# An encoder step on one core: every low-part subtraction of the output projections and of the plain gate/up tiles on VectorE

## Chip, cores and metric

The kernel runs on one NeuronCore of a Trainium2 chip (core 0, 16 DMA engines). The metric is the device time of one execution in microseconds. The median of three runs before the change is 2269.16 us (2268.02 to 2269.37). Engines in the text: TensorE (PE, with PEld for its weight loads), VectorE (DVE), ScalarE (ACT), GpSimd (POOL) and SyncE (SP), which issues the DMAs.

## The reference

Two layers run over 1056 rows (1024 prompt rows and 32 sample rows) of width 1024. Layer 0 mixes with an mLSTM, layer 1 with windowed attention with sinks and ALiBi; each has an output projection, a SwiGLU feed-forward part of width 2816 and two DeepNorm layer norms.

```python
def swiglu(x, w_gu, w_down):
    g, u = jnp.split(x @ w_gu, 2, axis=-1)
    return (jax.nn.silu(g) * u) @ w_down
...
for layer in range(DEPTH):
    if layer < N_A_LAYERS:
        mix, C, n, m = mlstm_mixer(x, w_in_a[layer], b_gate_a[layer], g_norm_a[layer], w_out_a[layer],
                                   C0s[layer], n0s[layer], m0s[layer])
    else:
        mix = swa_prompt(x, k_sh, v_sh, w_q_b[j], sinks_b[j], w_out_b[j], slopes)
    x = layer_norm(DEEPNORM_ALPHA * x + mix, ln_g[layer, 0], ln_b[layer, 0])
    x = layer_norm(DEEPNORM_ALPHA * x + swiglu(x, w_gu[layer], w_down[layer]), ln_g[layer, 1], ln_b[layer, 1])
```

## The kernel before

Activations lie transposed (feature on the partition) in `ACT` ("act" in the profile), 8 tiles of 128 features by 1056 columns. A product is formed from fp32r high and low parts: for every pair of tiles `gemm` issues three matmuls, high by high (L360), high by low (L361) and low by high (L362). `SX` ("sx") holds high and low parts of the activations; `split_act` makes them (ACT copies the high part at L390, DVE subtracts at L391), or the layer norm does (ACT L468; then L474, for even pairs of tiles on DVE, for odd ones on POOL).

Weights come through the class `Weights`. A unit is a tile of 128 x 1024; `load_to` issues its DMA on SP into one of three raw buffers ("wr", L159). Each unit has two halves, called factors 0 and 1, of 128 x 512. `_next` does the next half in a fixed order: ACT copies the high part (L200, into "wh"), then one engine subtracts it from the raw tile to give the low part (L202, into "wl"; or "ex"/"oh" where the half has a home in another buffer). This subtraction is called a split below. The engine of a split is chosen by one line: VectorE if (unit, factor) is in the set `on_vector`, GpSimd otherwise. Halves without a home share five slots. Most feed-forward tiles are in pairs with seven Strassen-like factors ("wl_a", "wl_b", "wl_s"), which the change does not touch.

`_next` is called while matmuls are written: `Weave.tick` counts the TensorE time issued so far and calls `feed`, and `split_to`/`factor` call it where a half is needed. The schedule is manual, so the order of the program text is the order on each engine's queue, and every engine runs its queue strictly in order.

Places at which the change acts:

- `mixer_out` with `U_OUT_A` (L1135 adds its products to act), after the mLSTM; `proj_o` with its chain of ACT L1034, DVE L1038, ACT L1040 and L1041, DVE L1043, L1044 and L1046 ends just before it, and its results are split at L390 and L391.
- `attention` with its stages scores (PE L1669/L1670, DVE L1675), soft (ACT L1687, DVE L1691, POOL L1693), turn (PE transposes L1713, ACT L1716, DVE L1717 writes "lo"), values (PE L1728/L1729), place (ACT L1737, DVE L1739). `mixer_out` with `U_OUT_B` begins while attention still runs.
- `up_plain`: the first FIRST = 2 gate/up tiles of each layer, once for each half of the columns (ACT silu L1251, DVE L1253). Meanwhile `ln_task` finishes the layer norm (DVE L426, L430, L447, L448, L452; POOL some of L430 and L474; PE L421 and L437), and `sums` makes sums of activations (DVE L1287 to L1293, ACT L1277, then L1274 alternating between POOL and DVE).

## Time and profile before

| | |
|---|---|
| median of 3 runs | 2269.16 us |
| the profiled execution | 2261.86 us |
| its span, first to last instruction | 2259.8 us |
| mean granted TensorE clock | 0.996 |
| DVE busy | 1490.3 us (66%) |
| ACT busy | 1015.3 us (45%) |
| POOL busy | 1135.6 us (50%) |

Durations below come from that one profiled execution. A row of the timeline gives the start in us from the span's start, the time in us, engine, line and operation, output and inputs, shapes and count, and in brackets the idle time of the engine before it and what ended it. In the table of waits a row reads: who waited, for whom, us in total, times, longest.

### The profile page before, as it was taken

Reading aid. Unit: us, or ns where it says so; the run is one execution under the profiler, and the core shown is the slowest. Engines: PE = TensorE matmul, PEld = TensorE weight load, DVE = VectorE, ACT = ScalarE, POOL = GpSimd, SP = SyncE. Lnnn points to the kernel's source line nnn. Section 1 sums busy time; section 2 is a strip of 40 time slices with the busy share of each in tenths; the row PEclk is TensorE's granted clock in tenths of the full one; section 3 lists DMA queues with packets and bytes.
Section 4 is the critical chain, followed back from the end, with each engine's and each line's share of the span. In section 5 each row is a group of like instructions: output and inputs, shape, how many; then the busy total and the mean of one; then the engine's idle time right before and its main releaser. Section 6 shows DMA issues by size and latency. Waiting matters only on the chain. (4 is left out here: it accounts for less than half of the span.)

```text
span 2259.8 us, 44187 instructions
## 1 busy us (share of the span) xinstructions
PE 2189.0 (97%) x17086; PEld 2149.0 (95%) x17086; DVE 1490.3 (66%) x2807; ACT 1015.3 (45%) x2285; POOL 1135.6 (50%) x1042
## 2 busy tenths in 40 slices
PE   9999999998999999999998999999999999999997
PEld 9899999998999999999997998899899999999997
DVE  4465577778666665566667778877666666466657
ACT  4443354455444444322246778756444444421124
POOL 2544333226666666544326776633666666554422
PEclk9999999999999999999999999999999999999999
DMA  4222112211434443697424211421343344397712
GB/s 148 74 54 69 53 39 85 96 39 66 150 137 153 158 143 139 219 333 234 162 79 138 85 60 44 137 72 47 115 152 140 135 146 163 124 334 259 248 57 77
DMA packets 167393, 291.52 MB, mean 129 GB/s; under 512 B 16592, under 2 KB 123144, under 8 KB 167184
## 3 DMA queue, kind: packets, MB, share of 16 engines
q1 hardware_dynamic: 162832, 284.38, 37.1%
q10 hardware_dynamic: 4352, 4.33, 0.5%
q8 instruction: 134, 2.20, 0.4%
q14 instruction: 75, 0.61, 0.1%
HBM read 203.89 MB, written 82.94 MB: 127 GB/s over the span
## 5 line engine op out<-in xcount | busy, mean ns | idle before, releaser
L202 POOL TENSOR_TENSOR wl_s<-wr,wh_s 128x512 fp32r<-128x512 f32 x224 | 316.8, 1435 | 241.3 <-ACT wh_s L200 158.2
L360 PE MATMUL d<-sx,wh 128*128 128x264 f32 (+2 forms) x1068 | 340.2, 319 | 1.2 <-DVE act L1505 0.7
L362 PE MATMUL d<-sx,wl 128*128 128x264 f32 (+2 forms) x1068 | 325.6, 305 | 8.4 <-DVE wl L202 6.0
L361 PE MATMUL d<-sx,wh 128*128 128x264 f32 (+2 forms) x1068 | 324.6, 304 | 3.8 <-DVE sx L474 2.6
L200 ACT CAST wh_s<-wr 128x512 fp32r<-128x512 f32 x224 | 135.5, 617 | 316.6 <-DVE wr L177 289.2
L360 PE MATMUL A<-sx,wh_s 128*128 128x264 f32 x896 | 254.6, 284 | 3.3 <-ACT z L1338 3.3
L202 POOL TENSOR_TENSOR wl<-wr,wh 128x512 fp32r<-128x512 f32 (+2 forms) x103 | 141.4, 1379 | 231.7 <-ACT wh L200 200.6
L361 PE MATMUL A<-sx,wh_s 128*128 128x264 f32 x896 | 254.2, 284 | 0.0
L362 PE MATMUL A<-sx,wl_s 128*128 128x264 f32 x896 | 254.0, 283 | 0.0
L362 PEld LDWEIGHTS d<-sx,wl 128*128 128x128 f32 x1068 | 200.9, 188 | 10.8 <-DVE wl L202 7.6
L361 PEld LDWEIGHTS d<-sx,wh 128*128 128x128 f32 x1068 | 201.6, 189 | 5.8 <-DVE sx L474 3.1
L360 PEld LDWEIGHTS d<-sx,wh 128*128 128x128 f32 x1068 | 201.7, 189 | 5.1 <-ACT z L443 1.1
L202 POOL TENSOR_TENSOR wl_a<-wr,wh_a 128x512 fp32r<-128x512 f32 x112 | 169.4, 1520 | 49.0 <-ACT wh_a L200 42.2
L362 PE MATMUL d<-sx,ex 128*128 128x264 f32 x624 | 178.5, 286 | 5.0 <-DVE ex L202 4.9
L360 PE MATMUL d<-sx,ex 128*128 128x264 f32 x624 | 181.0, 290 | 0.8 <-ACT sx L390 0.8
L361 PE MATMUL d<-sx,ex 128*128 128x264 f32 x624 | 178.2, 286 | 1.8 <-DVE sx L391 1.7
L360 PEld LDWEIGHTS A<-sx,wh_s 128*128 128x128 f32 x896 | 168.4, 188 | 3.7 <-ACT z L1338 3.7
L362 PEld LDWEIGHTS A<-sx,wl_s 128*128 128x128 f32 x896 | 168.9, 188 | 0.0
L361 PEld LDWEIGHTS A<-sx,wh_s 128*128 128x128 f32 x896 | 168.4, 188 | 0.0
L1208 POOL TENSOR_TENSOR z<-z 128x528 fp32r<-128x528 f32 x76 | 105.2, 1384 | 105.0 <-issue 53.2
L1693 POOL TENSOR_SCALAR s<-s,st 128x256 f32<-128x256 f32 (+1 forms) x144 | 124.2, 874 | 55.7 <-DVE st L1691 46.4
L1207 ACT CAST z<-z 128x528 fp32r<-128x528 f32 x136 | 85.8, 631 | 97.8 <-DVE z L1220 47.7
(334 smaller groups left out, 7404.2 us busy)
## 6 DMA issues: line engine op xcount, KB each, us to landing
wr<-in_gu SPq DMA_DIRECT2D x96, 512.0 KB, 4.5
hs_x<-z SPq DMA_DIRECT2D x72, 528.0 KB, 2.8
hs_t<-z SPq DMA_DIRECT2D x64, 528.0 KB, 4.1
sx<-hs_x SPq DMA_DIRECT2D x112, 264.0 KB, 6.0
sx<-hs_t SPq DMA_DIRECT2D x64, 264.0 KB, 6.0
ex<-hs_t SPq DMA_DIRECT2D x64, 264.0 KB, 6.2
wr<-in_dn SPq DMA_DIRECT2D x32, 512.0 KB, 5.2
ex<-hs_x SPq DMA_DIRECT2D x32, 264.0 KB, 6.1
```

The source lines that it names most:

```text
L200: self.nc.scalar.copy(hi, r)
L202: eng.tensor_sub(lo, r, hi.bitcast(F32))
L360: nc.tensor.matmul(out, ah, bh, start=start and k == 0, stop=False, **kw)
L361: nc.tensor.matmul(out, ah, bl, start=False, stop=False, **kw)
L362: nc.tensor.matmul(out, al, bh, start=False, stop=stop and k == last, **kw)
L1207: nc.scalar.copy(hi.bitcast(F32R), buf(s))
L1208: eng.tensor_sub(lo.bitcast(F32R), buf(s), hi)
L1693: nc.gpsimd.tensor_scalar_mul(p[:R, h, lo:256], p[:R, h, lo:256], st[:R, 2, h : h + 1])
```

## The change

Two lines that fill `on_vector` are changed; nothing is added beside them.

```diff
-        on_vector.update((u, 1) for i in range(FIRST) for c in range(2) for u in up[i, c])
+        on_vector.update((u, f) for i in range(FIRST) for c in range(2) for u in up[i, c] for f in range(2))
...
-    on_vector.update((u, 1) for u in U_OUT_A[0][3:] + U_OUT_B[0] + U_OUT_B[1])
+    on_vector.update((u, f) for u in U_OUT_A[0] + U_OUT_B[0] + U_OUT_B[1] for f in range(2))
```

43 splits of 128 x 512 leave POOL's queue and stand in DVE's: 11 of `U_OUT_A` (factor 0 of eight units, factor 1 of the first three), 16 of `U_OUT_B` (factor 0), and 8 of each layer's plain gate/up units (factor 0). The queues of PE, ACT and SP are the same row by row.

DVE at the end of `proj_o`, where mixer_out is about to begin (z_4627 is the scratch of the gates, ex_4623 the home of the output projection's halves):

```order
 L1046 TENSOR_SCALAR act<-act,gn,sg_4571 128x384
+L202 TENSOR_TENSOR ex_4623<-wr_4389,ex_4623 128x512 x2
 L1038 TENSOR_SCALAR z_4627<-z_4627 128x384
+L202 TENSOR_TENSOR ex_4623<-wr_4501,ex_4623 128x512
 L1043 TENSOR_TENSOR z_4627<-z_4627 128x384
 L1044 TENSOR_SCALAR z_4627<-z_4627 128x384
```

Splits now stand between the steps of the gate chain.

DVE in the last third of attention, one of six like places:

```order
 L1135 TENSOR_SCALAR act<-act,d_17093 128x264
 L202 TENSOR_TENSOR wl_1_17188<-wr_16036,wh_1_17187 128x512
+L202 TENSOR_TENSOR wl_0_17194<-wr_16945,wh_0_17193 128x512
 L1739 TENSOR_TENSOR act<-O_17162,t_17201 64x32 x2
 L1717 TENSOR_TENSOR lo_17207<-T_17205,hi_17206 128x512
```

Behind the split of one unit's second half now stands that of the next unit's first half, both ahead of L1739 and L1717.

DVE in layer 0's plain gate/up part, where the last quarter's layer norm ends:

```order
 L202 TENSOR_TENSOR wl_1_6153<-wr_5759,wh_1_6152 128x512
-L452 TENSOR_TENSOR act<-act,z_4627 128x2x264 x3
+L452 TENSOR_TENSOR act<-act,z_4627 128x2x264 x2
+L202 TENSOR_TENSOR wl_0_6184<-wr_6011,wh_0_6183 128x512
+L452 TENSOR_TENSOR act<-act,z_4627 128x2x264
 L474 TENSOR_TENSOR sx<-act,sx 128x2x264
 L1291 TENSOR_TENSOR z_4627<-act,z_4627 128x2x264
```

A split stands ahead of the last L452 and of L474. On POOL the same split stood ahead of a subtraction of `sums` (L1274) and of the two L474 of the odd pairs, which now follow the earlier POOL work directly. Layer 1 has the same rows.

## Prediction

> **What bounds the kernel now.** First the page's head and its first part.

> ```profile
> span 2259.8 us, 44187 instructions
> PE 2189.0 (97%) x17086; PEld 2149.0 (95%) x17086; DVE 1490.3 (66%) x2807; ACT 1015.3 (45%) x2285; POOL 1135.6 (50%) x1042
> ```

> PE is the bound; its whole idle time is 2259.8 - 2189.0 = 70.8 us. PE's queue is the same after the change, so the time can move only by what PE waits. Next the windows around the places of the change (start:end, length, then busy time of PE, PEld, DVE, ACT, POOL):

> ```profile
> 366.00:410.00 44.00, 40.69 (x274) 39.64 (x273) 35.89 (x54) 24.88 (x55) 17.31 (x12) 0.96 0.39 128
> 510.00:552.00 42.00, 35.97 (x279) 34.13 (x278) 38.57 (x42) 22.59 (x44) 27.34 (x17) 1.00 0.15 51
> 1370.00:1456.00 86.00, 76.32 (x587) 72.07 (x586) 76.99 (x260) 71.32 (x212) 56.93 (x63) 1.00 0.29 89
> 1456.00:1486.00 30.00, 27.99 (x228) 27.71 (x229) 23.60 (x38) 13.82 (x26) 14.41 (x10) 1.00 0.50 169
> 1558.00:1600.00 42.00, 35.95 (x280) 34.11 (x278) 38.57 (x41) 22.62 (x45) 27.98 (x18) 1.00 0.16 51
> ```

> I call them A (layer 0's output projection begins), C and C' (end of the plain gate/up part in layers 0 and 1), T (last part of attention) and B (layer 1's output projection). In C, C' and T DVE is busy for 90% or more (38.57 of 42; 76.99 of 86). The waits of PE in A (380 to 410), C (510 to 552), T (1370 to 1456) and B (1476 to 1486), in that order:

> ```profile
> PE d L361 <- DVE sx L391: 1.7, 2, 1.5
> PE d L360 <- ACT sx L390: 0.8, 1, 0.8
> PE d L362 <- DVE ex L202: 0.7, 1, 0.7
> ...
> PE d L362 <- DVE wl L202: 3.0, 3, 1.7
> PE d L361 <- DVE sx L474: 1.3, 1, 1.3
> ...
> PE d L361 <- POOL sx L474: 0.5, 1, 0.5
> ...
> PE T L1713 <- DVE lo L1717: 6.8, 5, 2.3
> PE T L1713 <- DVE st L1691: 1.7, 4, 0.7
> ...
> PE d L362 <- DVE ex L202: 2.0, 1, 2.0
> ```

> At all places PE waits for DVE. So the question is whether DVE's queue gets shorter or longer.

> **The change part by part.** A split on either engine (min/median/max ns):

> ```profile
> L202 POOL TENSOR_TENSOR wl<-wr,wh x103: 1010/1297/1833, 10.9 to 2161.7; 128x512 fp32r<-128x512 f32 x95, 128x544 fp32r<-128x544 f32 x4, 128x384 fp32r<-128x384 f32 x4
> L202 DVE TENSOR_TENSOR wl<-wr,wh x34: 551/692/1910, 5.1 to 2167.6; 128x512 fp32r<-128x512 f32 x30, 128x384 fp32r<-128x384 f32 x4
> ```

> POOL is rid of 43 x 1.30 = 56 us, which PE hardly waits for; DVE gets 43 x 0.69 = 30 us, about 0.6 each where instructions follow without a gap. But DVE does not work freely beside POOL's tensor operations. DVE's groups by shape in A (count, busy, mean ns) and rows of its timeline:

> ```profile
> L1044 DVE SCALAR_TENSOR_TENSOR z<-z 128x384 f32<-128x384 f32 x4 | 5.2, 1311 | 0.1
> L1046 DVE SCALAR_TENSOR_TENSOR act<-act,gn,z 128x384 f32<-128x384 f32 x4 | 4.4, 1090 | 0.1
> ...
> L1046 DVE SCALAR_TENSOR_TENSOR act<-act,gn,sg 128x384 f32<-128x384 f32 x1 | 1.5, 1451 | 0.1
> ...
> 385.66 3.17 POOL L202 TENSOR_TENSOR ex<-wr,ex 128x512 fp32r<-128x512 f32 x2 [3.92 <-ACT ex L200]
> ...
> 392.89 0.56 DVE L1044 SCALAR_TENSOR_TENSOR z<-z 128x384 f32<-128x384 f32 x1
> 393.49 0.62 DVE L1046 SCALAR_TENSOR_TENSOR act<-act,gn,z 128x384 f32<-128x384 f32 x1
> ...
> 389.77 0.39 PE L361 MATMUL d<-sx,ex 128*128 128x264 f32 x1 [1.51 <-DVE sx L391]
> ```

> The operations that take 0.56 and 0.62 us while POOL stands still take 1.31 and 1.09 on average: one that meets a POOL split (385.66 to 388.83 for two of them) loses up to 1 us, more than the 0.6 to 0.69 of doing the split itself. [...]

> *A.* Ahead of the L391 for which PE waits 1.51, DVE loses 4 x 0.75 + 4 x 0.47 + 0.8 = 5.7 us to the blocking; six added splits stand there, 6 x 0.62 = 3.7. So it comes 2.0 earlier, less what a split must wait for its cast: the 1.51 goes, and of the 0.8 and 0.7 about half stays. I take -1.9. Bounds: -3.2 (1.7 + 0.8 + 0.7), and +3.7 if the blocking stayed.

> *C and C'.* Here POOL's split waits for its cast, and POOL's later work waits behind it:

> ```profile
> 513.33 1.30 POOL L202 TENSOR_TENSOR wl<-wr,wh 128x512 fp32r<-128x512 f32 x1 [10.50 <-ACT wh L200]
> 514.59 1.32 POOL L1274 TENSOR_TENSOR ex<-z,ex 128x528 fp32r<-128x528 f32 x1
> ...
> 512.71 0.71 DVE L474 TENSOR_TENSOR sx<-act,sx 128x528 fp32r<-128x528 f32 x1 [0.46 <-ACT sx L468]
> 515.95 1.81 DVE L1291 TENSOR_TENSOR z<-act,z 128x528 f32<-128x528 f32 x1 [2.53 <-POOL ex L1274]
> 518.02 1.48 DVE L474 TENSOR_TENSOR sx<-act,sx 128x528 fp32r<-128x528 f32 x1
> 522.10 1.47 DVE L202 TENSOR_TENSOR wl<-wr,wh 128x512 fp32r<-128x512 f32 x1
> ...
> 517.25 0.39 PE L361 MATMUL d<-sx,wh 128*128 128x264 f32 x1 [0.49 <-POOL sx L474]
> ```

> The wait for the cast moves to DVE: its split starts at 513.33 too, and behind it in the queue stand the last L452 and the first L474, which ends at 513.33 + 3 x 0.7 = 515.4 instead of 513.4. PE wants that result six matmuls before 516.76 (517.25 - 0.49), at 0.129 us each (35.97/279): at 516.0, so 0.6 us of cover is left; without it this wait costs what is lacking, 1.8 at most. In return POOL's L1274 is done long before, L1291 no longer waits 2.53, and POOL's L474, for which PE waits at 517.25, comes up to 1.3 earlier. From 515.4 DVE has L1291, L1253 and its second L474 to do, three operations of at most 0.7, with some blocking by POOL's own L474 left: that L474 ends near 517.8 instead of 519.5, and the waits of 1.3 + 0.5 shrink to 0.4, which is -1.4. The last two of the eight added splits (0.69 each) stand where POOL splits blocked DVE by up to 1.0 each; the splits for which PE waits 3.0 so come a little earlier still, -0.9. I take -2.3 for each place, about half of 3.0 + 1.3 + 0.5 = 4.8. Bounds: -4.8, and +3.9 (three splits of 0.69 and 1.8 of waiting, nothing unblocked). The other five of each eight stand where PE has no wait in front of them; they cost nothing as long as the layer norm's L437 keeps its place in PE's queue.

> *T.* Six added splits stand ahead of L1739 and L1717, and PE's next transposes wait for L1717:

> ```profile
> 1429.83 0.69 DVE L1717 TENSOR_TENSOR lo<-T,hi 128x512 fp32r<-128x512 f32 x1
> 1440.22 1.91 DVE L202 TENSOR_TENSOR wl<-wr,wh 128x512 fp32r<-128x512 f32 x1
> ...
> 1440.30 1.28 POOL L202 TENSOR_TENSOR wl<-wr,wh 128x512 fp32r<-128x512 f32 x1
> ...
> 1430.67 0.63 PE L1713 MATMUL T<-ident,s 128*128 128x128 f32 x4
> 1443.49 0.33 PE L1713 MATMUL T<-ident,s 32*128 32x32 f32 x4 [1.02 <-DVE lo L1717]
> ```

> L1717 ends at 1430.52, PE transposes at 1430.67: no slack, so a split more is a wait of 0.6 more. I take the 0.6 at four of the six places and 0.4 at the first, where PE comes a little later than L1717; at the sixth POOL's split blocked DVE's (1.91 instead of 0.69), which falls away: -0.6. So 4 x 0.6 + 0.4 - 0.6 = +2.2, less 0.2 for an L391 that is no longer blocked: +2.0. Most other DVE work in T, L1717 among it, reads PSUM and shows no blocking, and POOL, busy 56.93 of 86, is relieved without use. Bounds: -1.7, the waits on L1691, if POOL's relief shortens the softmax chain; +4.1 (6 x 0.69) with no relief at all. [...]

> *B.* Weights arrive late:

> ```profile
> 1464.60 1.14 ACT L200 CAST ex<-wr 128x512 fp32r<-128x512 f32 x2 [3.23 <-DMA wr<-in_wout_b]
> ...
> 1481.00 1.75 DVE L202 TENSOR_TENSOR ex<-wr,ex 128x512 fp32r<-128x512 f32 x1
> ...
> 1482.81 0.39 PE L362 MATMUL d<-sx,ex 128*128 128x264 f32 x1 [2.01 <-DVE ex L202]
> ```

> The blocking of 1481.00 (1.75 against 0.69) goes, -1.0; but DVE's added splits wait for DMA and cast, with the layer norm's L426 and L430, L1135 and, through the raw buffers, SP's next weight loads behind them. I take -1.0; bounds -2.0 (the whole wait) and +3.2 (one such DMA wait passed on).

> Sum: -1.9 - 2.3 - 2.3 + 2.0 - 1.0 = -5.5 us, on a span of 2259.8: 2254.3. The profiled execution was 2261.86 (2.1 around the span), the median of the runs 2269.16, 7.3 above it; I add the difference to the median: **2263.7 us**.

> **Rivals.** *More gain.* If POOL's relief shortens T and the unblocked DVE gets ahead of PE in A and C: A -3.2, C and C' -4.0 each, B -1.0, T 0: -12.2, 2257.0. For it: DVE loses up to 1 us at every POOL split, and this falls away everywhere. Against: POOL's L1274 and L474 remain and still block.

> *No change.* In C and C' the wait for the cast on DVE eats what the unblocking gives (0 each): -5.5 + 4.6 = -0.9, 2268.3. For it: only 0.6 us of cover. Against: the 2.53 us for which L1291 waited for POOL is larger.

> *Slower.* In T DVE, busy for 76.99 of 86 us, becomes the engine that sets the pace: six splits at 0.69 go into PE's wait twice, since a late L1717 also delays the next scores and their return through ACT and POOL (8.3 us), and the splits behind it in B wait for DMA while the evacuations queue (+3.2). With A, C and C' at -6.5 that is +5.0: 2274.2. It decides as soon as T and B together cost over 6.5. For it: DVE's few gaps in T; against: by the order of the queues only every second transpose of T stands right behind such a split.

> That the splits move is seen in the order of the queues; nothing says that they would not.

> **How the numbers follow.** A measurement of this kernel tells about 0.2% (4.5 us) from no change. Forecast 0.42, more gain 0.15, no change 0.20, slower 0.23. The forecast lies only 1.0 beyond that bound: I count 0.33 of its 0.42 as faster. Faster 0.33 + 0.15 = 0.48; same 0.09 + 0.20 = 0.29; slower 0.23. The forecast's own range is 2259 to 2268 (T and C each off by 2 to 4); the range over the cases is 2255 to 2276.

> **What would show it.** DVE's L1044 and L1046 in A at 0.56 and 0.62 throughout, PE's 1.5 us wait for sx L391 gone. In C L1291 without its wait for POOL, DVE idle before the split for a cast, PE's waits for L474 under 0.5. In T more wait of PE for lo L1717, near 9 us instead of 6.8. In B a wait of about 1 instead of 2.0. DVE's busy time about the same, since 30 us come and the blocked shares go; POOL's 56 us less. I am wrong if DVE's rows stay as long as they are without POOL's splits, or if PE's wait in T grows by more than 5 us.

## The result and the profile after

The median fell from 2269.37 us (five runs, 2268.02 to 2272.42) to 2261.32 us (five runs, 2258.16 to 2262.37): ratio 0.9969, 95% interval 0.9959 to 0.998. A second comparison, of twelve runs against seventeen, gave 2262.2 against 2266.42: 0.9981, 0.9972 to 0.999. So the change is worth 4 to 7 us of 2266 (2 to 9 by the two intervals); 5.5 had been forecast.

The head of the page and its first part after the change:

```profile
span 2257.1 us, 44139 instructions
PE 2192.4 (97%) x17086; PEld 2152.2 (95%) x17086; DVE 1490.2 (66%) x2850; ACT 1016.2 (45%) x2285; POOL 1076.8 (48%) x999
```

DVE has 43 instructions more (2850 against 2807) and the same busy time (1490.2 against 1490.3): the 30 us of new splits replaced as much blocking. POOL has 58.8 us less. PE's idle time fell from 70.8 to 64.7. This profiled execution took 2258.92 us, near the fastest of its five; single spans say little here, for a reason that comes below.

The same windows as in the prediction (start:end, length, then PE, PEld, DVE, ACT, POOL, granted clock of PE, DMA share, GB/s); everything stands up to 6 us earlier now:

```profile
366.00:410.00 44.00, 43.32 (x311) 42.30 (x310) 36.66 (x74) 26.47 (x59) 0.52 (x1) 1.00 0.54 176
510.00:552.00 42.00, 36.55 (x281) 34.49 (x280) 37.74 (x42) 19.94 (x38) 26.75 (x17) 1.00 0.16 54
1370.00:1456.00 86.00, 75.85 (x564) 71.79 (x564) 76.53 (x261) 68.50 (x204) 46.13 (x53) 0.96 0.29 90
1456.00:1486.00 30.00, 30.00 (x245) 29.72 (x244) 24.96 (x46) 14.29 (x26) 1.33 (x1) 1.00 0.52 176
1558.00:1600.00 42.00, 36.51 (x281) 34.45 (x281) 38.23 (x42) 22.33 (x43) 25.64 (x16) 1.00 0.16 52
```

In A and B PE now works nearly without a stop (43.32 of 44, 30.00 of 30; before 40.69 and 27.99). In C and C' it gained 0.6, in T it lost 0.5, and T's granted clock is 0.96 instead of 1.00. PE's waits after the change, in A (380 to 410), C (505 to 546) and T (1366 to 1454); B has none:

```profile
PE d L360 <- ACT sx L390: 0.2, 1, 0.2
PE d L361 <- DVE sx L391: 0.2, 1, 0.2
PE d L360 <- DVE act L1135: 0.2, 1, 0.2
...
PE d L362 <- DVE wl L202: 2.8, 3, 1.2
PE A L360 <- ACT z L1321: 0.8, 1, 0.8
PE d L360 <- DVE z L1253: 0.7, 1, 0.7
PE d L361 <- DVE sx L474: 0.5, 1, 0.5
...
PE d L361 <- POOL sx L474: 0.2, 1, 0.2
...
PE T L1713 <- DVE lo L1717: 7.1, 5, 2.3
PE T L1713 <- DVE st L1691: 2.3, 4, 0.8
PE psS L1669 <- DVE st L1675: 0.7, 1, 0.7
```

A went from 3.2 to 0.6, B from 2.0 to nothing. In C the waits for L474 shrank from 1.8 to 0.7, but L1253, which PE had not waited for, now costs 0.7: 5.8 became 5.2. T went from 9.5 to 10.1.

**A second price of a wait.** PE's granted clock goes with the scatter of single spans: of the 17 runs of before in the second comparison, the fastest (2262.62 us) has a clock of 0.995 and the slowest (2271.88) one of 0.991. Two pairs of neighbouring windows of 3.41 us, the first pair from A before the change, the second from T after it:

```profile
388.74:392.15 3.41, 1.44 (x6) 0.91 (x6) 2.03 (x5) 2.10 (x5) 0.09 (x1) 1.00 0.68 216
392.15:395.56 3.41, 3.21 (x15) 3.12 (x15) 2.70 (x6) 1.34 (x4) 0.00 (x0) 0.50 0.28 81
```

```profile
1446.51:1449.92 3.41, 1.21 (x11) 1.13 (x11) 2.82 (x9) 2.46 (x9) 2.39 (x2) 1.00 0.43 154
1449.92:1453.33 3.41, 3.41 (x19) 3.08 (x18) 1.97 (x6) 1.61 (x7) 0.69 (x2) 0.50 0.27 53
```

PE is busy for 1.44 and 1.21 of 3.41 us in the first window of each pair, and in the next the clock is 0.50 for exactly that long. There the matmuls of 128x264 start every 0.22 us (before, 392.83 to 395.25), at full clock every 0.12 (395.64 to 397.11): by these two spacings an interval in which PE is busy throughout costs about 1.5 us more, an estimate. All such windows of an execution lie on one grid of 3.41 us (before they begin at 392.15, 1228.42 and 2252.41, 245 and 300 steps apart), whose position differs between executions, so the same wait sometimes falls into one interval and sometimes over two: of A's waits with the splits on POOL, 2.26 us fall into the interval from 387.82 in "B alone", and half clock follows; 1.55 into the one from 387.06 in "T alone", and none follows. I counted this in the thirteen profiles of this study, up to 2245 us, in intervals that were themselves at full clock: after an interval in which PE waited 1.86 us or more the next was at half clock in 32 of 32 cases; after 1.5 to 1.86 us in 27 of 72; after 1.3 to 1.5 in 4 of 33; after 1.2 to 1.3 in none of 18, nor after any shorter wait (rounding moves a case or two between the classes). Past 2245 us one case does not fit: before, PE waits 1.91 us from 2242.17 to 2245.58, and the next interval is at full clock. The most that a kernel can lose in this way is read from its runs: 1 minus the granted clock, times the span. Where PE waits anyway, half clock costs less than that (after the change PE is busy for 0.00 us of the half-clock interval from 1224.64). It is 16.7 to 17.7 us on average before the change (three sets of runs), and 14.1 to 14.5 after it. Of it 3.7 us (before) and 4.2 us (after) lie behind 2246 us, where PE has little left to do: it is busy there for 2.22 of 13.8 us before, at a clock of 0.73, and for 0.00 of 11.1 after, at 0.62.

### The profile page after: what moved, and what is told of

It is laid out like the page before. It is cut to its first block, busy times and chain, and to the rows that moved or that the text cites. A ratio compares the mean times of both kernels' runs of the same rounds, so it can differ in the third digit from the quotient of the medians.

```text
span 2257.1 us, 44139 instructions
## 1 busy us (share of the span) xinstructions
PE 2192.4 (97%) x17086; PEld 2152.2 (95%) x17086; DVE 1490.2 (66%) x2850; ACT 1016.2 (45%) x2285; POOL 1076.8 (48%) x999
## 4 chain that ended last, share of the span: by engine, by line
PE 80%; DVE 8%; ACT 4%; DMA 3%; issue 3%; POOL 1%; SPq 0%; ACTq 0%; DVEq 0%; POOLq 0%
PE A L360 9%; PE A L362 9%; PE A L361 9%; PE d L360 9%; PE d L362 9%; PE d L361 9%; PE B L360 7%; PE B L361 7%; PE B L362 7%; PE T L1713 1%; DMA sx<-hs_t 1%; DVE wl L202 1%; DMA wr<-in_dn 1%; DVE ex L1274 1%; PE T L904 1%
## 5 line engine op out<-in xcount | busy, mean ns | idle before, releaser
L202 POOL TENSOR_TENSOR wl_s<-wr,wh_s 128x512 fp32r<-128x512 f32 x224 | 316.6, 1434 | 241.0 <-ACT wh_s L200 169.0
L360 PE MATMUL d<-sx,wh 128*128 128x264 f32 (+2 forms) x1068 | 341.1, 319 | 2.2 <-DVE z L1253 1.5
L362 PE MATMUL d<-sx,wl 128*128 128x264 f32 (+2 forms) x1068 | 326.5, 306 | 7.7 <-DVE wl L202 5.5
L361 PE MATMUL d<-sx,wh 128*128 128x264 f32 (+2 forms) x1068 | 325.7, 305 | 2.0 <-DVE sx L474 1.1
L200 ACT CAST wh_s<-wr 128x512 fp32r<-128x512 f32 x224 | 135.4, 617 | 317.0 <-DVE wr L177 289.1
L360 PE MATMUL A<-sx,wh_s 128*128 128x264 f32 x896 | 255.2, 285 | 2.8 <-ACT z L1338 2.8
L361 PE MATMUL A<-sx,wh_s 128*128 128x264 f32 x896 | 254.8, 284 | 0.0
L362 PE MATMUL A<-sx,wl_s 128*128 128x264 f32 x896 | 254.7, 284 | 0.0
L362 PEld LDWEIGHTS d<-sx,wl 128*128 128x128 f32 x1068 | 201.7, 189 | 10.1 <-DVE wl L202 7.1
L360 PEld LDWEIGHTS d<-sx,wh 128*128 128x128 f32 x1068 | 202.4, 189 | 6.0 <-issue 2.2
L361 PEld LDWEIGHTS d<-sx,wh 128*128 128x128 f32 x1068 | 202.5, 190 | 4.3 <-POOL sx L474 1.5
L202 POOL TENSOR_TENSOR wl_a<-wr,wh_a 128x512 fp32r<-128x512 f32 x112 | 169.1, 1516 | 51.4 <-ACT wh_a L200 49.8
L202 POOL TENSOR_TENSOR wl<-wr,wh 128x512 fp32r<-128x512 f32 (+2 forms) x75 | 100.1, 1343 | 173.9 <-ACT wh L200 151.3
L360 PE MATMUL d<-sx,ex 128*128 128x264 f32 x624 | 180.7, 290 | 0.4 <-ACT sx L390 0.2
L362 PE MATMUL d<-sx,ex 128*128 128x264 f32 x624 | 177.9, 285 | 3.1 <-DVE ex L202 2.6
L361 PE MATMUL d<-sx,ex 128*128 128x264 f32 x624 | 177.3, 284 | 0.2 <-DVE sx L391 0.2
L360 PEld LDWEIGHTS A<-sx,wh_s 128*128 128x128 f32 x896 | 169.0, 189 | 3.3 <-ACT z L1338 3.3
L362 PEld LDWEIGHTS A<-sx,wl_s 128*128 128x128 f32 x896 | 169.4, 189 | 0.0
L361 PEld LDWEIGHTS A<-sx,wh_s 128*128 128x128 f32 x896 | 169.0, 189 | 0.0
L1693 POOL TENSOR_SCALAR s<-s,st 128x256 f32<-128x256 f32 (+1 forms) x144 | 125.5, 884 | 67.4 <-DVE st L1691 54.7
```

Of the source, the lines that this page charges most:

```text
L200: self.nc.scalar.copy(hi, r)
L202: eng.tensor_sub(lo, r, hi.bitcast(F32))
L360: nc.tensor.matmul(out, ah, bh, start=start and k == 0, stop=False, **kw)
L361: nc.tensor.matmul(out, ah, bl, start=False, stop=False, **kw)
L362: nc.tensor.matmul(out, al, bh, start=False, stop=stop and k == last, **kw)
L1693: nc.gpsimd.tensor_scalar_mul(p[:R, h, lo:256], p[:R, h, lo:256], st[:R, 2, h : h + 1])
```

## The experiments

In the table, "by ratio" is the ratio to before with its interval, times about 2266 us. The waits of PE are those of one profile at the five places; where a half-clock interval falls into a place, PE arrives later there and waits less (C in "A alone" and "T alone", C' in "B alone", 4.5). So a place at which nothing was changed still differs from profile to profile: A from 2.3 to 4.4, and B, with T unchanged too, from 1.2 to 2.1. "Half clock" is that upper bound, the mean over the runs, with that of the before beside it.

| kernel | ratio (95%) | by ratio | A, C, T, B, C' | half clock (before) |
|---|---|---|---|---|
| before | | | 3.2, 5.8, 9.5, 2.0, 5.9 | |
| changed, first | 0.9969 (0.9959 to 0.998) | -7.0 | 0.6, 5.2, 10.1, 0, 5.5 | 14.5 |
| changed, again | 0.9981 (0.9972 to 0.999) | -4.3 | 0.4, 5.3, 10.1, 0.2, 5.4 | 14.1 (16.7) |
| A alone | 0.9983 (0.9974 to 0.9991) | -3.9 | 0.6, 4.5, 9.4, 1.8, 5.8 | 16.2 (17.0) |
| C, C' alone | 0.9993 (0.9984 to 1.0001) | -1.6 | 2.3, 5.3, 9.5, 1.2, 5.5 | 15.2 (17.0) |
| T alone | 1.0023 (1.0013 to 1.0032) | +5.2 | 4.4, 4.5, 10.0, 3.4, 5.7 | 20.1 (17.0) |
| B alone | 0.9991 (0.9982 to 0.9999) | -2.0 | 3.1, 5.7, 9.0, 1.0, 4.5 | 16.2 (17.0) |
| without T | 0.9964 (0.9953 to 0.9976) | -8.2 | 0.6, 5.3, 9.0, 0.4, 5.5 | 12.8 (16.7) |
| with needless matmuls | 0.9963 (0.995 to 0.9976) | -8.4 | 0.6, 5.3, 7.1, 0, 5.6 | 7.7 (16.7) |
| L1274 on DVE too | 0.9945 (0.9934 to 0.9957) | -12.5 | 0.6, 2.7, 10.9, 0, 2.7 | 14.0 (16.7) |
| L1274 alone | 0.9979 (0.997 to 0.9988) | -4.8 | 3.2, 3.6, 8.8, 2.1, 3.4 | 18.5 (17.7) |
| T's splits all on POOL | 0.9961 (0.9949 to 0.9974) | -8.8 | 0.6, 5.3, 7.7, 0, 5.5 | 14.0 (17.7) |
| all that helped | 0.9934 (0.9921 to 0.9946) | -15.0 | 0.6, 4.3, 6.6, 0, 2.8 | 9.0 (17.7) |

### Four parts, one at a time

Part A:

```diff
-    on_vector.update((u, 1) for u in U_OUT_A[0][3:] + U_OUT_B[0] + U_OUT_B[1])
+    on_vector.update([(u, 1) for u in U_OUT_A[0][3:] + U_OUT_B[0] + U_OUT_B[1]] + [(u, f) for u in U_OUT_A[0] for f in range(2)])
```

> Only the 11 splits of layer 0's output projection are moved to VectorE. Places are named as in the prediction; the waits of PE in the profile decide, since the median moves by little more than its scatter. Theory L (the parts act each at its own place, by the sizes that the trace of the changed kernel shows): A's waits of PE fall from 3.2 to 0.6 us, C, C', T and B keep 5.8, 5.9, 9.5 and 2.0; PE's idle time is 2.6 below the 70.8 of before; median 2.6 below. Theory P (the terms of the prediction): A's waits fall by 1.9, to 1.3. Theory W (POOL's relief as a whole counts, not the place): A's waits fall by less than 1 when the other 32 splits stay on POOL.

A's waits fell to 0.6, as theory L had it and more than the forecast's 1.9. By ratio it is 3.9 us (2.0 to 5.9), the waits being 2.6: the difference fits the half clock that follows A's 1.5 us wait (392.15 above) in four of the five profiles with A's splits on POOL, and in none of the eight with them on DVE.

Parts C and C':

```diff
-        on_vector.update((u, 1) for i in range(FIRST) for c in range(2) for u in up[i, c])
+        on_vector.update((u, f) for i in range(FIRST) for c in range(2) for u in up[i, c] for f in range(2))
```

> Only the 16 splits of the plain gate/up units are moved to VectorE. Theory L: in C and C' the wait for L474 shrinks by about 1.3 each and is given back at the later splits and at L1253, where VectorE has no gap left: waits 5.8 to 5.2 and 5.9 to 5.5, together -1.0; median within 0.1% of before. Theory P: -2.3 in each, so waits of 3.5 and 3.6, together -4.6, median 4.6 below. A, T and B keep 3.2, 9.5 and 2.0.

5.8 and 5.9 became 5.3 and 5.5: theory L. The 4.6 of the forecast is outside the interval (-3.6 to +0.2).

Part T, then part B (the same line as for A, with `U_OUT_B[0]` or `U_OUT_B[1]` in its second list):

> Only the eight splits of the first pass over layer 1's output projection (T) are moved. Theory L: T's waits go from 9.5 to about 10.1, +0.6; B may lose part of its 2.0, nothing else. Theory P: +2.0, T's waits about 11.5, and L1717's share 9 instead of 6.8. A rival in which the half-speed stretches of PE in T come from the moved splits: T loses 3 us or more, with a granted clock near 0.66 in two stretches of 5 us between 1410 and 1456.

T alone makes the kernel slower, by more than any theory's waits. T's own waits rose by only 0.5 (9.5 to 10.0). But B now waits 3.4 instead of 2.0, and both places are followed by half clock. PE's waits in B of this kernel, the longest wait of ACT there before and in this kernel, and PE's windows behind the last wait of T and behind that of B:

```profile
PE d L362 <- DVE ex L202: 2.2, 1, 2.2
PE d L362 <- POOL ex L202: 1.0, 1, 1.0
PE d L362 <- DVE wl L202: 0.2, 1, 0.2
```

```profile
1464.60 1.14 ACT L200 CAST ex<-wr 128x512 fp32r<-128x512 f32 x2 [3.23 <-DMA wr<-in_wout_b]
...
1479.60 1.86 ACT L200 CAST ex<-wr 128x512 fp32r<-128x512 f32 x3 [6.42 <-DMA wr<-in_wout_b]
```

```profile
1458.85:1462.26 3.41, 3.41 (x19) 3.08 (x18) 1.83 (x6) 1.50 (x6) 0.82 (x2) 0.50 0.24 44
1492.98:1496.39 3.41, 3.41 (x15) 3.41 (x16) 2.69 (x6) 0.00 (x0) 0.00 (x0) 0.50 0.71 203
```

T's last wait for L1717 was 1.60 before and is 2.20 now: 0.6 more, but past the 1.86 from which half clock followed in every counted case. In B ACT waits 6.42 us for weights instead of 3.23; SP had waited 6.6 us for a split of DVE, which frees the raw buffer, before it issued that load (5.1 before). This is the path that the prediction feared for B (+3.2), here in one profile of a kernel that moved nothing in B. Waits in T and B are up by 1.9 (one profile each) and half clock by 3.0 (20.1 against 17.0, over all runs), together 4.9 of the measured 5.2. The rival in which half clock comes with the moved splits is borne out in the time, through the waits, but only in part at its places. Of the stretches at 1424.71, 1458.85 and 1492.98 in this profile, the first has its like at 1418 to 1422 in three profiles whose T splits were not moved; the second follows T's last wait. Without needless matmuls, that wait was followed by half clock in three of four profiles with T's splits moved, in two of seven without.

> Only the eight splits of the second pass over layer 1's output projection (B) are moved. Theory L: PE's wait of 2.0 goes wholly, median 2.0 below. Theory P: half of it stays, -1.0. If the whole wait goes only because T's splits were moved too (POOL's queue then reaches B earlier), 1 or more of it stays here.

Half of the wait stayed, 1.0, as the forecast had it; but "C, C' alone", which moved nothing in B, shows 1.2, so one profile cannot tell what B's splits did to it. In the kernels that moved A, B and C together it is 0 to 0.4, with T's splits moved or not; so the last of those theories, that T's move frees B, does not hold. What frees the rest of B there stays open.

### The changed kernel again, and without T

No edit in the first; in the second the first list of the line keeps `U_OUT_B[0]` and the second has `U_OUT_A[0] + U_OUT_B[1]`.

> The changed kernel itself, once more, as the base for the three beside it. Ratio to before 0.9969, about 7 us. In the traces so far PE runs at half speed in whole stretches of 3.41 us (392.15 to 395.56 before; 579.53, 1415.79 and 1449.92 after), all on one grid of 3.41 us whose phase differs from execution to execution, and each follows a grid interval in which PE's waits came to 1.56 us or more. Theory H (waits close together cost a second time, through half speed): the time lost at half speed, worked out for each run as 1 minus the granted clock, times the span, is 14.5 us on average here against 17.0 before. Theory N (half speed comes by chance): no difference between the kernels over some ten runs.

14.1 us at half clock against 16.7, as theory H had it. The scatter of the runs leaves 2.5 +- 2.6 us, so this pair alone does not decide against theory N; the needless matmuls below do.

> All of the change but T: U_OUT_B's first pass keeps its eight splits on POOL. The single parts gave -2.8 (A and with it nothing else, median), -2.1 (C), -1.1 (B) and +5.9 (T) against the before of the same chip. If they add up: 6 below before, and so 6 below all_moved, which would be level with before. If T costs only what its waits show (10.1 instead of 9.5 us): within 1 us of all_moved. Theory H: T's last wait stays at 1.6 instead of 2.2 us, so that fewer half-speed stretches follow, 0.6 x 1.7 us less; together 1.5 to 3 us below all_moved.

T's waits are 9.0 and its last one 1.61; half clock is 12.8 us. By the two ratios the kernel is 3.9 us faster than the changed one beside it, although their intervals overlap. Whether the parts add up cannot be told: the four single medians make about nothing and the four ratios -2.3, the whole gives 4 to 7, each part being uncertain by about 2. A, C and B alone make -7.5, near the -8.2 of the kernel without T. T cost 5.2 alone and some 4 in company, where B's waits are gone.

### Needless matmuls in PE's waits

```diff
+fill = lambda n: n and (lambda ps: [nc.tensor.matmul(ps[:, :256], KH[0][:, :P], KH[0][:, :256], start=True, stop=True) for _ in range(n)])(psbank())
...
-            kc = slice(k0, k0 + 256 - lo)
+            kc = slice(k0, k0 + 256 - lo); fill(40 * (ast["scored"] == 1))
...
-            kts = key_tiles(b)
+            kts = key_tiles(b); fill({(5, 6): 12, (6, 3): 8, (7, 7): 12}.get((j, b), 0))
```

> The changed kernel with 72 needless matmuls put on PE's queue (128x256 into a spare bank), ahead of four of its waits in attention: 40 ahead of the wait of 5.61 us at 1228.10, 12, 8 and 12 ahead of those of 2.32, 1.56 and 2.20 us in T. They stand where PE waits anyway, about 0.11 us each (four L1728/L1729 in 0.47 us), and no other engine's queue changes. Theory H: the half-speed stretches at 1224 to 1231 and in T go; the time lost at half speed falls by 3.4 + about 2, and the median by 1.7 (the half of the first that lies outside the wait) + 2, 2.5 to 4 us in all, although PE does more work. Theory N: median the same or up to 1 us later, and as much half speed as before.

The window from 1220 to 1236, of the changed kernel's first profile and of this kernel:

```profile
1220.00:1236.00 16.00, 10.35 (x61) 9.71 (x60) 11.50 (x35) 11.94 (x35) 11.66 (x14) 0.79 0.52 159
```

```profile
1220.00:1236.00 16.00, 15.23 (x107) 14.23 (x106) 12.32 (x36) 12.78 (x36) 12.62 (x15) 1.00 0.54 172
```

The clock is 1.00 there instead of 0.79 (0.89 in the changed kernel's second profile), and in T no half-clock window is left. Half clock fell from 14.1 to 7.7 us per run, far outside the scatter, and the median by 3.0 (by the ratios 4.1, their intervals overlapping), with 72 matmuls more. The time fell by less than the half clock. That is theory H: the queues of the other engines are the same, and only PE's idle time was filled. So PE's waits cause the half clock; that the limit lies at 1.86 is counted, not tested.

### What blocks DVE in C

```diff
-                        (nc.vector if s & 1 else nc.gpsimd).tensor_sub(d[:, 1], bufs[s % 2], d[:, 0].bitcast(F32))
+                        nc.vector.tensor_sub(d[:, 1], bufs[s % 2], d[:, 0].bitcast(F32))
```

> The changed kernel with the even L1274 of sums on VectorE too, so that POOL has no tensor operation left in C and C' but L474 and L430. Theory B (VectorE in C is slowed by POOL's L1274, which block its two-input operations for 1 us and more): a moved L1274 costs 0.7 and frees about 1.1, C's waits fall from 5.2 to 4 or less, median 1 to 3 us lower. Theory D (VectorE is simply full in C): each moved L1274 adds its 0.7 to VectorE's queue, C's waits rise to 6.5 or more, median 2 us higher or more.

The waits in C halved, from 5.3 to 2.7, and the median fell 7.9 us below the changed kernel beside it: theory B, and more than the 1 to 3 us that it had. The waits at the five places fell by 4.5 (21.4 to 16.9) and half clock stayed (14.0 against 14.1), so some 3 of the 7.9 are not accounted for here. In C of the changed kernel the timeline shows why the moved splits had not brought this. DVE, then POOL:

```profile
507.74 0.69 DVE L202 TENSOR_TENSOR wl<-wr,wh 128x512 fp32r<-128x512 f32 x1 [1.60 <-ACT wh L200]
...
509.58 1.84 DVE L1291 TENSOR_TENSOR z<-act,z 128x528 f32<-128x528 f32 x1
...
512.30 1.82 DVE L1274 TENSOR_TENSOR ex<-z,ex 128x528 fp32r<-128x528 f32 x1
514.15 1.72 DVE L1287 TENSOR_TENSOR z<-act 128x528 f32<-128x528 f32 x1
```

```profile
509.31 1.54 POOL L474 TENSOR_TENSOR sx<-act,sx 128x528 fp32r<-128x528 f32 x1 [6.20 <-ACT sx L468]
511.92 1.64 POOL L474 TENSOR_TENSOR sx<-act,sx 128x528 fp32r<-128x528 f32 x1 [1.06 <-ACT sx L468]
513.52 1.78 POOL L1274 TENSOR_TENSOR ex<-z,ex 128x528 fp32r<-128x528 f32 x1
```

L1291 meets POOL's L474 and ends at 511.42, 0.57 after it (509.31 + 1.54 = 510.85); L1274 and L1287 meet the second L474 and POOL's L1274 and end 0.56 and 0.57 after them. Each loses 1.0 to 1.1. DVE's groups in C (505 to 548) in the changed kernel and in this one:

```profile
L1274 DVE TENSOR_TENSOR ex<-z,ex 128x528 fp32r<-128x528 f32 x6 | 8.7, 1446 | 0.0
L1287 DVE TENSOR_TENSOR z<-act 128x528 f32<-128x528 f32 x3 | 4.1, 1375 | 0.1
```

```profile
L1274 DVE TENSOR_TENSOR ex<-z,ex 128x528 fp32r<-128x528 f32 x12 | 10.6, 885 | 0.0
L1287 DVE TENSOR_TENSOR z<-act 128x528 f32<-128x528 f32 x3 | 2.1, 706 | 0.1
```

Twelve of these L1274 on DVE take 1.9 us more than six did, and the L1287 beside them lost their blocking.

> The kernel before, with none of the 43 splits moved, but the even L1274 (16 in all, eight in each layer) on VectorE. It tells which of POOL's operations held VectorE back in C. Theory S (the splits did, and L1274 is the smaller part): C's waits fall from 5.8 to 5 or less but stay well above the 2.7 of the kernel with both moved; median 1 to 3 us below before. Theory L1274 (that one did, and the splits hardly matter): C's waits fall to about 3 by this alone, median 5 to 7 below before. Theory D (VectorE full): C's waits rise to 7 or more.

Between the two theories, nearer the second: L1274 alone takes C from 5.8 to 3.6 (-2.2), the splits alone took it to 5.3 (-0.5), both together to 2.7 (-3.1, or -2.6 from the changed kernel).

### T the other way round, and all together

The line is that of the kernel without T, and its first list loses `U_OUT_B[0]` as well, so that all 16 of T's splits are POOL's.

> All of the change but T, and in T the other way round: all 16 splits of U_OUT_B's first pass on POOL, the eight that VectorE had before too. T's waits are 9.0 us with eight splits on either engine and 10.1 with 16 on VectorE. Theory F (VectorE sets T's pace, POOL's splits do not block what it reads from PSUM): a split less is 0.6 us less at each place where PE waits for L1717; T's waits fall to 6 or 7, median 2 to 4 below the kernel with eight on POOL (0.9964 of before, so 0.995). Theory K (POOL's splits block L391 and one another, and come late behind POOL's L1693): T's waits stay at 9 or rise, PE waits for splits of POOL by L362, median the same or higher.

T's waits, in the window 1360 to 1466:

```profile
PE T L1713 <- DVE lo L1717: 3.6, 3, 1.6
PE T L1713 <- DVE st L1691: 1.5, 3, 0.7
PE T L1713 <- POOL s L1693: 1.4, 4, 0.6
PE psS L1669 <- DVE st L1675: 1.2, 2, 0.9
```

The waits for L1717 halved, from 6.8 to 3.6, as theory F had it; 1.4 came back as waits for POOL's L1693. The sum is 7.7 against 9.0. In the time, 0.9961 cannot be told from the 0.9964 of the kernel with eight on each engine; the 2 to 4 us of theory F are not seen.

The last kernel is "without T", with L1274 on DVE and 34, 12, 5 and 7 needless matmuls:

> All that helped, together: the change without T, L1274 wholly on VectorE, and needless matmuls ahead of PE's waits in attention (34 ahead of the one of 5.5 us, 12, 5 and 7 ahead of those of 2.33, 1.31 and 1.61 in T). If the gains add up against before: -8.0 (without T), -7.9 (L1274, against the changed kernel beside it), -3.0 (needless matmuls, likewise): 2247.5 us on a median of 2266.4, ratio 0.9917. If T and the needless matmuls overlap, since both take half-speed stretches from T: 2249, ratio 0.992. If waits only change their place (the sequence from POOL to VectorE turns round): no better than 0.9945.

2250.46 us against 2267.99, the fastest kernel here. It is 4 us short of the full sum; the second estimate (0.992) and the third (0.9945) both lie at the edges of its interval, which also overlaps that of "L1274 on DVE too". Half clock, 9.0 us, is not below the 7.7 of the needless matmuls alone: this fits the second estimate, that T's splits and they take away the same. In this profile the split that waited 0.6 in C with L1274 moved waits 2.1, so part of the rest is waits that moved:

```profile
PE d L362 <- DVE wl L202: 2.1, 1, 2.1
PE d L361 <- DVE sx L474: 1.9, 1, 1.9
```

## Why the prediction was right, and where not

The total, 5.5 us less, lies between the two measured gains (4.3 and 7.0). That is in part luck: of the 5.0 us by which the waits fell, C and C' gave 3.6 less than forecast, and A, T and B 3.1 more; the half clock was not in the sum.

**A, -1.9: right in kind, too small.** DVE's groups in A (361 to 404) after the change:

```profile
L1046 DVE SCALAR_TENSOR_TENSOR act<-act,gn,z 128x384 f32<-128x384 f32 x4 | 2.5, 619 | 0.1
L1044 DVE SCALAR_TENSOR_TENSOR z<-z 128x384 f32<-128x384 f32 x4 | 2.2, 557 | 0.1
```

They are as short as foretold (1090 and 1311 before), and the 1.5 us wait is 0.2. The residue is 0.6 of 3.2, so -2.6; the prediction had left "about half" of the waits on ACT and the split. By ratio, with the half clock behind it, A was worth 3.9.

**C and C', -2.3 each: mis-sized; the runs show -0.5 each in waits.** The first half of the step held: the split waits for its cast on DVE (1.60), L1291 no longer waits for POOL, and PE's waits for L474 shrank by 1.1. The step that failed is "the last two of the eight added splits stand where POOL splits blocked DVE by up to 1.0 each; the splits for which PE waits 3.0 so come a little earlier still, -0.9". Two rows of POOL and of DVE, before and then after:

```profile
530.28 1.67 POOL L202 TENSOR_TENSOR wl<-wr,wh 128x512 fp32r<-128x512 f32 x1 [1.89 <-issue]
530.72 1.80 DVE L1274 TENSOR_TENSOR ex<-z,ex 128x528 fp32r<-128x528 f32 x1
...
524.71 1.83 POOL L1274 TENSOR_TENSOR ex<-z,ex 128x528 fp32r<-128x528 f32 x1 [3.10 <-ACT ex L1277]
525.27 1.83 DVE L1274 TENSOR_TENSOR ex<-z,ex 128x528 fp32r<-128x528 f32 x1
```

The blocking by the split was read rightly, but when the split went, POOL's next L1274 stood in its place and blocked the same operation as long (1.83 against 1.80). So the added splits cost their 0.6 each without return, the wait for splits stayed at 2.8, and L1253 became a wait. The rival of no change had C and C' at 0, nearer to this, but put it down to the wait for the cast.

**T, +2.0: too large in waits (+0.6), too small in time (about +4 in company, by overlapping intervals, and +5.2 alone).** L1717 was to cost near 9 us and costs 7.1. DVE's groups in T (1396 to 1454), before and after, show what was overlooked:

```profile
L391 DVE TENSOR_TENSOR sx<-act,sx 128x384 fp32r<-128x384 f32 x9 | 5.9, 654 | 0.3 <-ACT sx L390 0.2
L202 DVE TENSOR_TENSOR wl<-wr,wh 128x512 fp32r<-128x512 f32 x7 | 6.2, 888 | 0.1
```

```profile
L391 DVE TENSOR_TENSOR sx<-act,sx 128x384 fp32r<-128x384 f32 x9 | 5.0, 550 | 0.2 <-ACT sx L390 0.2
L202 DVE TENSOR_TENSOR wl<-wr,wh 128x512 fp32r<-128x512 f32 x14 | 9.3, 700 | 0.1
```

Seven more splits cost 3.1 us, not 7 x 0.69 = 4.8, and nine L391 give 0.9 back where 0.2 was allowed for one. But the last wait passed 1.86 us, and the half clock that followed was in no term. In T the splits were better left on POOL: the kernel without T's moves has 0.9964 against 0.9981, and T alone 1.0023. The forecast's sum without its +2.0 for T, -7.5, is near the measured -8.2. In A (waits from 3.2 to 0.6) and with L1274 (C's waits from 5.3 to 2.7) the blocking decides the other way.

**B, -1.0: what the one profile of B alone shows; -2.0 in company.** The feared waits took place without PE noticing: in the changed kernel ACT waits 2.91 us for a weight load and DVE's split 1.45 for ACT, but DVE waited as long before (1.51). In T alone, where the load came later, PE did notice.

**Missing altogether: half clock, 14.1 against 16.7 us per run.** The waits fell by 5.0 at the five places, the half clock by 2.5 (uncertain by 2.6); behind A's wait it went, behind T's last wait it came.

## What to carry over

When an operation is moved from POOL to DVE to end blocking, list every POOL operation left in that stage: in C moving one kind freed almost nothing (waits from 5.8 to 5.3 us), since the next kind blocked as much (1.83 us for an L1274 of DVE, 1.80 before). Price a wait of PE by its place too: in this kernel 1.9 us and more within one interval of 3.41 us brought half clock in the next (32 of 32 cases up to 2245 us), about 1.5 us for a busy PE, so that by this count two waits of 1 us in different intervals are cheaper than one of 2. Independent needless matmuls in waits that stayed took much of that second price away here: 7.7 us at half clock per run instead of 14.1.

## What the hardware showed unexpectedly

A DVE operation with two operands in SBUF that started while POOL worked on two tensors (L202, L474, L1274) did most of its work after it. One of 128x528 ends 0.56 to 0.57 us after POOL's (0.70 alone; three cases in C above, and before the change 26 of the 27 L474, L1274, L1287 and L1291 that started so; the other began 0.04 us before POOL's end), one of 128x384 0.42 after it (0.56 alone; in A before, L1044 at 380.56 takes 1.60 and POOL's split ends at 381.74). Operations that read PSUM showed none of this: the four L1717 of 128x512 that started so before the change took 0.69 us, as they do alone. POOL's L1693, a multiplication by a scalar and nearly its only work left in T, hardly does this: DVE's splits took 0.67 to 0.91 us in T after the change (0.69 alone).
